# Grouped-MoE routing of a two-layer diffusion backbone: selection by pairwise comparison, row stores issued by SyncE

## The chip, the cores and the metric

The kernel runs on one core of a Trainium2 chip. The metric is the device time of one launch in microseconds (us); the kernel before takes 1316.8 us, the median of three runs (1316.08 to 1317.06). The engines are TensorE (PE), VectorE (DVE), ScalarE (ACT), GpSimd (POOL) and SyncE (SP). Each of them has a queue of instructions that it serves in order; DMAs are issued from such a queue, and in this kernel nearly all loads are issued by SP.

## The reference

Two layers run over 256 context tokens and 256 latent tokens of width 1024. A layer modulates its stream, projects it, runs two mixers (a gated linear recurrence and a neighbourhood attention), projects back with `w_out`, adds and normalizes, and then applies a mixture of 16 experts, which chooses two per token:

```python
def grouped_moe(h, w_router, b_router, w_gate_l, w_up_l, w_down_l):
    t = h.reshape(-1, shp[-1])                                   # tokens x 1024
    aff = sigmoid(t @ w_router)                                  # tokens x 16
    sel = (aff + b_router).reshape(n, 4, 4)                      # 4 groups of 4 experts
    group_score = lax.top_k(sel, 2)[0].sum(-1)                   # sum of the two best of each group
    g_idx = argmax(group_score)                                  # one group per token
    in_grp = sel[token, g_idx]
    local = lax.top_k(in_grp, 2)[1]                              # the two best experts of that group
    e_idx = g_idx * 4 + local
    gates = aff[e_idx] / sum(aff[e_idx])
    for e in range(16):                                          # w_gate, w_up 1024x512, w_down 512x1024
        hid = silu(t @ w_gate_l[e]) * (t @ w_up_l[e])
        out += combine[:, e:e+1] * (hid @ w_down_l[e])
```

Before it, `x = layer_norm(ALPHA*x + g1*y)` and `h = x*(1+sc2)+sh2`; behind it, another gated residual and layer norm. Layer 1 needs the latent tokens alone.

## The kernel before, in words

Tokens are treated in halves of 256: half 0 is the context, half 1 the latent tokens. Layer 0 has both, the first half's end overlapping the second half's matmuls; layer 1 has half 1 alone. Weights come in tiles of 1 MB (128 partitions x 2048 f32). Matrices that need precision are split into a high and a low part and multiplied in three matmuls (lines 426 to 428).

*Output projection.* For each half and each column tile of `w_out`, PE fills the bank `psy`, DVE adds the result to x, and `settle` (line 982) follows one column tile behind: `stat` accumulates sums of x and x squared by matmul into the bank `st`, and then x, scaled on ACT, is transposed by matmuls into the four banks `tr`. At the end of a half `owed` is emptied, one column tile after the other, each with its sums and its transposes.

*`ln1_end` (lines 1095 to 1145).* From `st` come mean and variance, from them the router's logits (`lg`), `aff`, and a small matrix `rT`. PE adds one matmul to each of the four `tr` banks, whose contents are then rows of h up to a factor. ACT evicts three of them to `hr` (line 1131), DVE the one of (n, j) = (1, 0) (line 1129), and each is stored to DRAM, to `hD`, from ACT's queue (line 1132).

*`route` (from 1148).* DVE computes which two experts each token takes: 25 small instructions on tiles of 128 x 16, 128 x 8 or 128 x 32 elements (lines 1170 to 1196, `sel` to `oh1`, `oh2` and their sum `m16`). PE counts places by a triangular matmul (`ppos`), DVE builds one-hot tiles (`oh`, line 1227, called `t` in the first half), PE turns them into lists of tokens (`ptb`, line 1231), and DVE writes these as `gidx` and `sums` (lines 1235, 1236). `by_load` sorts all but a few of the experts by load.

*`moe` (from 1304).* For each expert POOL gathers its rows of h from `hD` by an indirect DMA (`gather`, line 1345) into `xg`; the gather of a row needs both the indices and the stores. PE transposes them (`ptx`, line 1354), multiplies by gate and up (`pgA`, `pgB`, lines 1369 and 1379), then down (lines 1406 and 1412); POOL scatters the result (line 1433). Weights go to 16 slots of 1 MB, named `we` and `mw` after their pools; an expert takes four for gate and up (`in_wgu_dram`) and two for down (`in_wd_dram`), loaded by SP (line 1335). Of the first round, the slots from number NFREE on (14 in layer 0, 13 in layer 1) are held back: before their load POOL copies one element of the first gathered tile into the slot (line 1326), so the load follows the landing of the first gather. `fl` and `pfl` (lines 1521, 1523) are a flag on the last expert and its matmul.

What sets the order: a scheduler places the instructions of all engines when the kernel is built, from their dependencies; the order of the code decides among those that it could choose. Each engine then serves its queue in the order that came out.

Of the kernel before, what the change touches and what calls it, by code (L numbers as in the profile page):

```python
# [11 lines left out]
I32 = mybir.dt.int32  # L12
AF = mybir.ActivationFunctionType
# [5 lines left out]
P = 128  # L19
# [42 lines left out]
for _name, _w in (("sel4", 32), ("ident", 128), ("m0", 64), ("m1", 64), ("m2", 64), ("m4", 64), ("m8", 64), ("mM", 64),  # L62
                  ("cos", 256), ("sin", 256), ("tok", 4), ("c4", 8),
                  ("c32", 32), ("ord", 3 * NSORT), ("tri", 128), ("iota", CAP), ("rowtok", SEQ)):
    _C[_name] = (_n, _n + _w)
    _n += _w
# [4 lines left out]
def const_table():  # L71
# [28 lines left out]
    put("c32", np.broadcast_to(np.tile([4, 3, 2, 1], 8), (P, 32)))  # L100
# [85 lines left out]
class Emit:  # L186
# [740 lines left out]
    def w_out(self, l):  # L927
# [52 lines left out]
        def settle(xs, hf, st, tr, seen):  # L980
            self.stat(st, xs, seen)
# [14 lines left out]
        for half, c in order:  # L996
# [33 lines left out]
            if len(owed) > 1:  # L1030
                settle(*owed.pop(0))
            if (half, c) == order[0]:
                rows_of_g()
            if c == order[3 if hf == order[0][0] else -1][1]:
                while owed:
                    settle(*owed.pop(0))
# [56 lines left out]
    def ln1_end(self, hf, st, tr):  # L1093
# [29 lines left out]
        for n in range(2):  # L1123
            for j in range(2):
# [3 lines left out]
                if (n, j) == (1, 0):  # L1128
                    V.tensor_scalar(hr[:], tr[2 * n + j][:], s[:, 3, n:n + 1], None, op0=ALU.mult)
                else:  # L1130
                    S.activation(hr[:], tr[2 * n + j][:], AF.Copy, scale=s[:, 3, n:n + 1])
                S.dma_start(self.hD[128 * (n0 + n):128 * (n0 + n) + 128, 512 * j:512 * j + 512], hr[:])
# [14 lines left out]
    def route(self, hf, n0, aff):  # L1147
# [5 lines left out]
        sel, w1, w2 = (rt([P, 2, NE], x) for x in ("sel", "w1", "w2"))  # L1153
# [3 lines left out]


        grp = lambda x: x.rearrange("p t (g x) -> p (t g) x", g=4)
        s4 = sel[:].rearrange("p t (g x y) -> p (t g) x y", g=4, x=2)  # L1160
        gg = rt([P, 6, 8, 2], "gg")
        fl = lambda i, y: gg[:, i, :, y]
        wide = lambda x: x.unsqueeze(2).to_broadcast([P, 8, 4])
        t4 = lambda x: x.rearrange("p (t g) -> p t g", t=2)
        gm = rt([P, 4, 2], "gm")
        b4 = lambda x: x.unsqueeze(2).to_broadcast([P, 2, 4])
        g1 = rt([P, 2, NE], "g1")
        s44, wa, wb, wc = grp(sel[:]), grp(w1[:]), grp(w2[:]), grp(g1[:])
        c32 = self.cst("c32").rearrange("p (g x) -> p g x", x=4)
        V.tensor_tensor(gg[:, 0], s4[:, :, 0, :], s4[:, :, 1, :], op=ALU.max)  # L1170
        V.tensor_tensor(gg[:, 1], s4[:, :, 0, :], s4[:, :, 1, :], op=ALU.min)
        V.tensor_tensor(fl(2, 0), fl(0, 0), fl(0, 1), op=ALU.max)
        V.tensor_tensor(fl(2, 1), fl(0, 0), fl(0, 1), op=ALU.min)
        V.tensor_tensor(fl(3, 0), fl(1, 0), fl(1, 1), op=ALU.max)
        V.tensor_tensor(wa, s44, wide(fl(2, 0)), op=ALU.is_ge)
        V.tensor_tensor(fl(3, 0), fl(3, 0), fl(2, 1), op=ALU.max)
        V.tensor_tensor(wa, wa, c32, op=ALU.mult)
        V.tensor_tensor(fl(3, 1), fl(2, 0), fl(3, 0), op=ALU.add)
        V.tensor_reduce(fl(5, 0), wa, axis=AX.X, op=ALU.max)
        V.tensor_reduce(gm[:, 0], t4(fl(3, 1)), axis=AX.X, op=ALU.max)  # L1180
        V.tensor_tensor(wa, wa, wide(fl(5, 0)), op=ALU.is_equal)
        V.tensor_tensor(t4(fl(4, 0)), t4(fl(3, 1)), b4(gm[:, 0]), op=ALU.is_ge)
        V.scalar_tensor_tensor(wb, wa, -3e38, s44, op0=ALU.mult, op1=ALU.add)
        V.tensor_tensor(fl(4, 0), fl(4, 0), self.cst("c4"), op=ALU.mult)
        V.tensor_tensor(wb, wb, wide(fl(3, 0)), op=ALU.is_ge)
# [583 lines left out]
```

## Time and profile before

| | |
|---|---|
| median of 3 runs | 1316.8 us |
| the profiled execution's own time | 1317.83 us |
| its span | 1316.1 us |
| mean granted clock of TensorE | 0.958 |
| PE, PEld busy | 1199.3 us (91%), 747.6 us (57%) |
| DVE, ACT, POOL busy | 590.2 us (45%), 413.8 us (31%), 334.4 us (25%) |
| moved by DMA | 339.32 MB, mean 258 GB/s |

All times of rows are counted from the start of the span of one profiled execution, which took 1.0 us more than the median. PEld is the load of a matmul's weights, which overlaps PE. In a timeline, several instructions of one kind stand in one row (x8) with their common time; an engine's name with a q (SPq, ACTq) is the issue of a DMA from its queue; a bracket tells how long the engine was idle before, and which instruction or DMA released it as far as the semaphores show. "DMA to landing" is the time from the start of an issuing instruction's transfer to its completion. In a table of stretches, the granted clock stands as a share of 2.4 GHz (0.50 is 1.2 GHz), and the DMA share is the busy time of 16 DMA engines.

### The profile page before, as it was taken

What the parts mean: (1) busy time and instruction counts of PE and PEld (TensorE: products, weight loads), DVE (VectorE), ACT (ScalarE), POOL (GpSimd) and SP (SyncE); (2) the same over time, 40 slices, a digit from 0 to 9 for tenths busy, and PEclk for the clock granted to TensorE, in tenths of its full rate; (3) what the DMA queues carried; (4) which work ended last, traced back from release to release, by engine and by line L of the source; (5) the groups of instructions that cost most, each with busy time, mean ns of one, the idle gap of its engine ahead of it and who ended that gap; (6) DMA issues with size and microseconds to landing.
All of it is one profiled execution on the core that took longest, in us unless ns stands there. A gap on an engine that the chain in (4) does not pass through costs nothing. (4 is left out here: it accounts for less than half of the span.)

```text
span 1316.1 us, 22763 instructions
## 1 busy us (share of the span) xinstructions
PE 1199.3 (91%) x8919; PEld 747.6 (57%) x8919; DVE 590.2 (45%) x1397; ACT 413.8 (31%) x905; POOL 334.4 (25%) x349
## 2 busy tenths in 40 slices
PE   6989999988999799998997999998889899999984
PEld 4778767667788334333332688876667734333321
DVE  2466554786735414121111756364785524322214
ACT  2233254452544114111112653354345312001011
POOL 2233243323223101111000534353343311111001
PEclk9999999999999799999998999998999889999996
DMA  8794325313385799999998524354335799999993
GB/s 299 250 313 189 122 89 197 116 52 108 124 332 188 266 374 375 386 395 384 412 404 298 227 101 167 115 192 152 131 116 213 314 352 380 389 404 402 421 413 151
DMA packets 67684, 339.32 MB, mean 258 GB/s; under 512 B 10003, under 2 KB 17907, under 8 KB 31856
## 3 DMA queue, kind: packets, MB, share of 16 engines
q1 hardware_dynamic: 54016, 315.74, 62.1%
q0 software_dynamic: 5936, 12.58, 2.9%
q10 hardware_dynamic: 7616, 9.44, 2.2%
q8 instruction: 74, 1.21, 0.4%
q14 instruction: 42, 0.34, 0.1%
HBM read 322.80 MB, written 20.45 MB: 261 GB/s over the span
## 5 line engine op out<-in xcount | busy, mean ns | idle before, releaser
L422 POOL TENSOR_TENSOR wl<-w,wh 128x512 fp32r<-128x512 f32 x121 | 166.4, 1389 | 188.5 <-ACT wh L421 171.7
L1369 PE MATMUL pgA<-we,xgT 128*64 128x512 f32 x688 | 165.2, 613 | 2.7 <-DMA we<-in_wgu_dram 2.7
L426 PE MATMUL pscm<-xh,wh 128*128 128x512 f32 (+1 forms) x320 | 119.1, 376 | 3.3 <-ACT wh L421 2.3
L427 PE MATMUL pscm<-xl,wh 128*128 128x512 f32 (+1 forms) x320 | 120.7, 379 | 0.7 <-POOL xl L1603 0.5
L428 PE MATMUL pscm<-xh,wl 128*128 128x512 f32 (+1 forms) x320 | 118.6, 375 | 2.8 <-POOL wl L422 2.6
L421 ACT ACTIVATE wh<-w 128x512 fp32r<-128x512 f32 x160 | 96.5, 626 | 50.4 <-PE pscm L427 18.7
L1369 PEld LDWEIGHTS pgA<-we,xgT 128*64 128x64 f32 x688 | 48.1, 140 | 95.1 <-issue 84.9
L427 PE MATMUL pstm<-wl,xh 128*128 128x256 f32 x320 | 92.6, 290 | 3.4 <-DVE wl L422 1.8
L428 PE MATMUL pstm<-wh,xl 128*128 128x256 f32 x320 | 91.9, 287 | 0.0
L426 PE MATMUL pstm<-wh,xh 128*128 128x256 f32 x320 | 91.6, 287 | 0.0
L1433 POOL DMA_INDIRECT yD<-y,ss x25 | 23.0, 921 | 244.6 <-DVE y L1421 79.9
L1406 PE MATMUL pdA<-we,hdT 128*64 128x512 f32 x320 | 77.6, 619 | 3.3 <-DMA we<-in_wd_dram 3.2
L1369 PE MATMUL pgA<-mw,xgT 128*64 128x512 f32 x336 | 77.5, 598 | 0.0
L1360 DVE COPY xgT<-ptx 128x256 f32<-128x256 f32 (+1 forms) x32 | 15.4, 482 | 134.2 <-PE ptx L1354 91.1
L426 PEld LDWEIGHTS pscm<-xh,wh 128*128 128x128 f32 x320 | 61.3, 193 | 13.8 <-ACT wh L421 2.4
L428 PEld LDWEIGHTS pscm<-xh,wl 128*128 128x128 f32 x320 | 61.5, 193 | 12.5 <-POOL wl L422 3.4
L427 PEld LDWEIGHTS pscm<-xl,wh 128*128 128x128 f32 x320 | 61.9, 194 | 11.2 <-POOL xl L1603 1.6
L1387 DVE SCALAR_TENSOR_TENSOR hid<-hid,pgA 128x256 f32<-128x256 f32 x32 | 13.5, 421 | 115.2 <-ACT hid L1386 115.1
L427 PEld LDWEIGHTS pstm<-wl,xh 128*128 128x128 f32 x320 | 61.4, 192 | 5.4 <-POOL wl L422 2.2
L1386 ACT ACTIVATE hid<-pgA 128x256 f32<-128x256 f32 x32 | 12.3, 383 | 159.5 <-PE pgA L1369 159.5
L428 PEld LDWEIGHTS pstm<-wh,xl 128*128 128x128 f32 x320 | 61.5, 192 | 1.1 <-issue 0.8
L426 PEld LDWEIGHTS pstm<-wh,xh 128*128 128x128 f32 x320 | 61.4, 192 | 0.5
(394 smaller groups left out, 2358.9 us busy)
## 6 DMA issues: line engine op xcount, KB each, us to landing
we<-in_wgu_dram SPq DMA_DIRECT2D x86, 1024.0 KB
mw<-in_wgu_dram SPq DMA_DIRECT2D x42, 1024.0 KB
w<-in_wada_dram SPq DMA_DIRECT2D x41, 1024.0 KB
we<-in_wd_dram SPq DMA_DIRECT2D x40, 1024.0 KB
w<-in_win_dram SPq DMA_DIRECT2D x29, 1024.0 KB
mw<-in_wd_dram SPq DMA_DIRECT2D x24, 1024.0 KB
w<-in_wout_dram SPq DMA_DIRECT2D x11, 1024.0 KB
wa<-in_wada_dram SPq DMA_DIRECT2D x6, 1024.0 KB
```

The lines of the kernel that those rows point to most:

```text
L421: self.nc.scalar.activation(hi, src, AF.Copy)
L422: leng.tensor_tensor(lo, src, hi.bitcast(F32), op=ALU.subtract)
L426: mm(out, lh, rh, start=first, stop=False, **k)
L427: mm(out, lh, rl, start=False, stop=False, **k)
L428: mm(out, ll, rh, start=False, stop=last, **k)
L1360: V.tensor_copy(t[:, 0:4, :c], src)
L1369: mm(pA[64 * j:64 * j + 64, :], xgT[e][:, k, 0:64], wk[:, 512 * j:512 * j + 512], start=(k == 0), stop=(k == KT - 1), skip_group_check=Tru ...
L1386: S.activation(h, ps[:, :n], AF.Tanh, scale=0.5)
L1387: V.scalar_tensor_tensor(h, h, 1.0, ps[:, :n], op0=ALU.add, op1=ALU.mult)
L1406: mm(dA[64 * j:64 * j + 64, :], hdT[e][:, kb, 0:64], wk[:, 512 * j:512 * j + 512], start=(kb == 0), stop=(kb == 3), skip_group_check=True, ...
L1433: G.indirect_dma_start(out=self.yD[l][:], out_offset=bass.IndirectOffsetOnAxis(ap=idx, axis=0), in_=y[:c], in_offset=None, bounds_check=2 ...
```

## The change

- The selection is rewritten. Each expert is compared with the four of its group at once: two compares over 128 x (8 groups x 4 x 4) elements, "greater" and "greater or equal"; the latter replaces the former where the other expert stands earlier in the group (the constant `before`, which takes the place of `c32`), and the sum over the four is the expert's rank. The two of rank below 1.5 are the top two, their masked sum is the group's score, and the best group is found as before with `c4`. `m16` and `oh2` come straight from the rank, and `oh1` is their difference. There are 14 instructions instead of 25.
- All four rows of h of a half are evicted by ACT, and their stores are issued by SP instead of ACT.
- `settle` takes a list: at the end of a half the sums of all owed column tiles come ahead in the code of all their transposes, which are now in `turns`.
- The temporary tiles `w1` that `w3` and the last expert's flag use are now called `top`.

```diff
 _n = 0
 for _name, _w in (("sel4", 32), ("ident", 128), ("m0", 64), ("m1", 64), ("m2", 64), ("m4", 64), ("m8", 64), ("mM", 64),
                   ("cos", 256), ("sin", 256), ("tok", 4), ("c4", 8),
-                  ("c32", 32), ("ord", 3 * NSORT), ("tri", 128), ("iota", CAP), ("rowtok", SEQ)):
+                  ("before", 16), ("ord", 3 * NSORT), ("tri", 128), ("iota", CAP), ("rowtok", SEQ)):
     _C[_name] = (_n, _n + _w)
     _n += _w
 NCONST = _n
...
     put("iota", np.broadcast_to(np.arange(1, CAP + 1), (P, CAP)))
     put("tok", i[:, None] + 128 * np.arange(4)[None, :] - BIG)
     put("c4", np.broadcast_to(np.tile([4, 3, 2, 1], 2), (P, 8)))
-    put("c32", np.broadcast_to(np.tile([4, 3, 2, 1], 8), (P, 32)))
+
+    put("before", np.broadcast_to((np.arange(4)[None, :] < np.arange(4)[:, None]).reshape(-1), (P, 16)))
     put("sel4", (s % 32) == np.arange(32)[None, :])
     o = np.arange(NSORT)
     put("ord", np.broadcast_to(np.concatenate([o[::-1], o, o + NSTAT]), (P, 3 * NSORT)))
...
             self.R.update(uv=uv, gbr=gbr)
 
 
-        def settle(xs, hf, st, tr, seen):
-            self.stat(st, xs, seen)
+        def settle(jobs):
+            for xs, hf, st, tr, seen in jobs:
+                self.stat(st, xs, seen)
+            for job in jobs:
+                turns(*job)
+
+        def turns(xs, hf, st, tr, seen):
             for m, x, _ in xs:
                 rs = rt([P, 256], "rs", 2)
                 S.activation(rs[:], x, AF.Copy, scale=gb[:, m, 2 * hf:2 * hf + 1])
...
                 xs.append((m, x, w32[:, hf, m, :]))
             owed.append((xs, hf, st, tr, seen))
             if len(owed) > 1:
-                settle(*owed.pop(0))
+                settle([owed.pop(0)])
             if (half, c) == order[0]:
                 rows_of_g()
             if c == order[3 if hf == order[0][0] else -1][1]:
-                while owed:
-                    settle(*owed.pop(0))
+                settle(owed)
+                owed = []
                 if hf == 0:
                     self.ln1_end(hf, st, tr)
         return st, tr
...
                 hr = rt([P, 512], "hr", 4)
                 mm(tr[2 * n + j][:], rT[0:12, 128 * n:128 * n + 128], R["gbr"][0:12, 512 * j:512 * j + 512], start=False, stop=True,
                    skip_group_check=True)
-                if (n, j) == (1, 0):
-                    V.tensor_scalar(hr[:], tr[2 * n + j][:], s[:, 3, n:n + 1], None, op0=ALU.mult)
-                else:
-                    S.activation(hr[:], tr[2 * n + j][:], AF.Copy, scale=s[:, 3, n:n + 1])
-                S.dma_start(self.hD[128 * (n0 + n):128 * (n0 + n) + 128, 512 * j:512 * j + 512], hr[:])
+                S.activation(hr[:], tr[2 * n + j][:], AF.Copy, scale=s[:, 3, n:n + 1])
+                nc.sync.dma_start(self.hD[128 * (n0 + n):128 * (n0 + n) + 128, 512 * j:512 * j + 512], hr[:])
         if l == 1:
...
         NTL = self.T * P
         mm = nc.tensor.matmul
         ns = slice(n0, n0 + 2)
-        sel, w1, w2 = (rt([P, 2, NE], x) for x in ("sel", "w1", "w2"))
+        sel, rank = (rt([P, 2, NE], x) for x in ("sel", "rank"))
         oh1, oh2, gt = R["oh1"][:, ns], R["oh2"][:, ns], R["gt"]
         V.tensor_scalar(aff[:], aff[:], 0.5, 0.5, op0=ALU.mult, op1=ALU.add)
         V.tensor_tensor(sel[:], aff[:], self.br[:].unsqueeze(1).to_broadcast([P, 2, NE]), op=ALU.add)
 
-
         grp = lambda x: x.rearrange("p t (g x) -> p (t g) x", g=4)
-        s4 = sel[:].rearrange("p t (g x y) -> p (t g) x y", g=4, x=2)
-        gg = rt([P, 6, 8, 2], "gg")
-        fl = lambda i, y: gg[:, i, :, y]
-        wide = lambda x: x.unsqueeze(2).to_broadcast([P, 8, 4])
-        t4 = lambda x: x.rearrange("p (t g) -> p t g", t=2)
-        gm = rt([P, 4, 2], "gm")
-        b4 = lambda x: x.unsqueeze(2).to_broadcast([P, 2, 4])
-        g1 = rt([P, 2, NE], "g1")
-        s44, wa, wb, wc = grp(sel[:]), grp(w1[:]), grp(w2[:]), grp(g1[:])
-        c32 = self.cst("c32").rearrange("p (g x) -> p g x", x=4)
-        V.tensor_tensor(gg[:, 0], s4[:, :, 0, :], s4[:, :, 1, :], op=ALU.max)
-        V.tensor_tensor(gg[:, 1], s4[:, :, 0, :], s4[:, :, 1, :], op=ALU.min)
...
-        V.tensor_tensor(grp(oh1), wa, wide(fl(4, 1)), op=ALU.mult)
-        V.tensor_tensor(wb, wb, wide(fl(5, 1)), op=ALU.is_equal)
-        V.tensor_tensor(wc, wa, wb, op=ALU.add)
+        s4 = grp(sel[:])
+        by_j, by_i = s4.unsqueeze(2).to_broadcast([P, 8, 4, 4]), s4.unsqueeze(3).to_broadcast([P, 8, 4, 4])
+        cmp = self.mt([P, 256], "adasb", 4)
+        gt4, ge4 = (cmp[:, 128 * i:128 * i + 128].rearrange("p (g i j) -> p g i j", g=8, i=4) for i in range(2))
+        gt3, ge3 = (cmp[:, 128 * i:128 * i + 128].rearrange("p (g x) -> p g x", g=8) for i in range(2))
+        V.tensor_tensor(gt4, by_j, by_i, op=ALU.is_gt)
+        V.tensor_tensor(ge4, by_j, by_i, op=ALU.is_ge)
+        V.copy_predicated(gt3, self.cst("before").unsqueeze(1).to_broadcast([P, 8, 16]).bitcast(I32), ge3)
+        V.tensor_reduce(grp(rank[:]), gt4, axis=AX.X, op=ALU.add)
+
+        gg = rt([P, 3, 8], "gg")
+        gm = rt([P, 2, 2], "gm")
+        top = rt([P, 2, NE], "top")
+        t4 = lambda i: gg[:, i].rearrange("p (t g) -> p t g", t=2)
+        b4 = lambda i: gm[:, i].unsqueeze(2).to_broadcast([P, 2, 4])
+        V.scalar_tensor_tensor(top[:], rank[:], 1.5, sel[:], op0=ALU.is_lt, op1=ALU.mult)
+        V.tensor_reduce(gg[:, 0], grp(top[:]), axis=AX.X, op=ALU.add)
+        V.tensor_reduce(gm[:, 0], t4(0), axis=AX.X, op=ALU.max)
+        V.tensor_tensor(t4(1), t4(0), b4(0), op=ALU.is_ge)
+        V.tensor_tensor(gg[:, 1], gg[:, 1], self.cst("c4"), op=ALU.mult)
+        V.tensor_reduce(gm[:, 1], t4(1), axis=AX.X, op=ALU.max)
+        V.tensor_tensor(t4(2), t4(1), b4(1), op=ALU.is_equal)
+        mine = gg[:, 2].unsqueeze(2).to_broadcast([P, 8, 4])
 
         m16 = R["m16"]
-        V.tensor_tensor(grp(m16[:, ns]), wc, wide(fl(4, 1)), op=ALU.mult)
-        V.tensor_tensor(grp(oh2), wb, wide(fl(4, 1)), op=ALU.mult)
+        V.scalar_tensor_tensor(grp(m16[:, ns]), grp(rank[:]), 1.5, mine, op0=ALU.is_lt, op1=ALU.mult)
+        V.scalar_tensor_tensor(grp(oh2), grp(rank[:]), 1.0, mine, op0=ALU.is_equal, op1=ALU.mult)
+        V.tensor_tensor(oh1, m16[:, ns], oh2, op=ALU.subtract)
         pp = self.pb("ppos")
         for n in range(n0, n0 + 2):
             o = pp[:, NE * (n - n0):NE * (n - n0) + NE]
```

SP's queue around the routing of layer 0, before (`w_45` is the last tile of `w_out`, `we` and `mw` are slots of weights):

```order
L199 DMA w_45_4338<-in_wout_dram 128x2048
L1335 DMA we<-in_wgu_dram 128x2048 x5
L1335 DMA we<-in_wd_dram 128x2048 x2
L1335 DMA mw<-in_wgu_dram 128x2048 x4
L1335 DMA mw<-in_wd_dram 128x2048 x2
```

and after; the first four `hr` are the rows of the first half, the next four those of the second:

```order
L1135 DMA hD<-hr_3989 128x512
L1135 DMA hD<-hr_3993 128x512
L1135 DMA hD<-hr_3997 128x512
L1135 DMA hD<-hr_4001 128x512
L1328 DMA we<-in_wgu_dram 128x2048 x2
L1328 DMA we<-in_wd_dram 128x2048 x2
L1135 DMA hD<-hr_4465 128x512
L1135 DMA hD<-hr_4469 128x512
L1135 DMA hD<-hr_4473 128x512
L1135 DMA hD<-hr_4477 128x512
L1328 DMA mw<-in_wgu_dram 128x2048 x4
L1328 DMA mw<-in_wd_dram 128x2048 x2
```

The stores now stand in SP's queue, the second four of them ahead of four loads of gate and up weights and of the two held-back loads of down weights.

SP's queue around the routing of layer 1, before:

```order
L199 DMA w_81_10113<-in_wout_dram 128x2048
L1335 DMA we<-in_wgu_dram 128x2048 x8
L1335 DMA we<-in_wd_dram 128x2048 x2
L1335 DMA mw<-in_wgu_dram 128x2048 x3
L1335 DMA mw<-in_wd_dram 128x2048 x2
```

and after:

```order
L1328 DMA we<-in_wgu_dram 128x2048 x8
L1328 DMA we<-in_wd_dram 128x2048
L1135 DMA hD<-hr_10229 128x512
L1135 DMA hD<-hr_10233 128x512
L1135 DMA hD<-hr_10237 128x512
L1135 DMA hD<-hr_10241 128x512
L1328 DMA we<-in_wd_dram 128x2048
L1328 DMA mw<-in_wgu_dram 128x2048 x3
L1328 DMA mw<-in_wd_dram 128x2048 x2
```

The four stores stand ahead of the second load of the down weights and of the three gate and up loads, of which the last is held back.

PE's queue in layer 1 from the last of the index matmuls to the first expert, before:

```order
L1231 MATMUL ptb<-rr_10320,oh 96x2
L1523 LDWEIGHTS one_97
L1523 MATMUL pfl<-fl_1_11043,one_97 128x1
L1354 MATMUL ptx<-ct,xg_10410 128x96 x8
L1369 MATMUL pgA<-we,xgT_10423 64x512 x8
L1379 MATMUL pgB<-we,xgT_10423 32x256 x16
```

and after:

```order
L1224 MATMUL ptb<-rr_10287,oh 96x2
L1347 MATMUL ptx<-ct,xg_10377 128x96 x8
L1516 LDWEIGHTS one_97
L1516 MATMUL pfl<-fl_1_11010,one_97 128x1
L1362 MATMUL pgA<-we,xgT_10390 64x512 x8
L1372 MATMUL pgB<-we,xgT_10390 32x256 x16
```

The flag's matmul moves behind the eight transposes of the first gathered tile; the rest stands as it did.

At the ends of both halves that a routing waits for, PE's sums (`st`) and transposes (`tr`) stand in the order that they had. In the first half of layer 0, `ppos` stands six matmuls earlier, and a pair of transposes now lies among the matmuls of `ptb`.

## Rows read from the trace of the kernel before

**Rows 1.** Chain of waits, 1180 to 1300 us: share of each kind of piece.
```profile
by line: DMA we<-in_wgu_dram 33.9%; DMA mw<-in_wgu_dram 18.7%; DMA mw<-in_wd_dram 16.9%; DMA we<-in_wd_dram 13.5%; PE pdA L1406 6.2%; PE pgA L1369 5.8%; PE pfin L1658 1.7%; issue 1.3%; DVE zt L1646 0.7%; DVE y L1421 0.6%; PE ptx L1354 0.5%;
```

**Rows 2.** Stretches: length, busy of PE, PEld, DVE, ACT, POOL, PEclk, DMA, GB/s.
```profile
430.00:434.50 4.50, 2.01 (x10) 1.16 (x11) 3.52 (x30) 1.36 (x4) 0.70 (x1) 1.00 1.01 428
439.00:445.00 6.00, 2.25 (x27) 2.15 (x25) 4.77 (x24) 0.00 (x0) 2.40 (x2) 0.50 0.21 54
...
460.00:560.00 100.00, 100.00 (x805) 39.93 (x793) 28.58 (x61) 24.81 (x56) 10.52 (x11) 1.00 1.00 378
1066.00:1188.00 122.00, 122.00 (x930) 47.68 (x929) 37.24 (x77) 16.38 (x43) 15.14 (x16) 1.00 1.00 391
```

**Rows 3.** Timeline of SP, layer 0: start, duration, instruction.
```profile
421.33 0.85 SPq L1335 DMA_DIRECT2D mw<-in_wgu_dram  x2
...
425.96 0.33 SPq L1335 DMA_DIRECT2D mw<-in_wgu_dram  x1
...
445.24 0.90 SPq L1335 DMA_DIRECT2D mw<-in_wd_dram  x2
```

**Rows 4.** Timeline of POOL, layer 0, with idle time before and its releaser.
```profile
440.54 1.44 POOL L1345 DMA_INDIRECT xg<-hD,gidx  x1 [9.21 <-DVE sums L1236]
...
445.01 0.34 POOL L1326 COPY mw<-xg 96x1 f32<-96x1 f32 x2 [1.78 <-DMA xg<-hD,gidx]
```

**Rows 5.** Timeline of PE, layer 0, first transposes of the expert stage.
```profile
445.09 1.51 PE L1354 MATMUL ptx<-ct,xg 96*128 96x96 f32 x8 [2.06 <-DMA xg<-hD,gidx]
```

**Rows 6.** Timeline of DVE, layer 0, selection to indices.
```profile
432.70 0.17 DVE L1170 TENSOR_TENSOR gg<-sel 128x16 f32<-128x16 f32 x1
...
435.99 0.19 DVE L1195 TENSOR_TENSOR m<-g,gg 128x32 f16<-128x32 f32 x1
...
438.01 0.16 DVE L1235 TENSOR_TENSOR gidx<-ptb,sums 96x2 int32<-96x2 f32 x1
```

**Rows 7.** Timeline of ACT, layer 0, evictions and stores of h.
```profile
433.74 1.26 ACT L1131 ACTIVATE hr<-tr,lnst 128x512 f32<-128x512 f32 x2 [0.64 <-PE tr L1126]
434.45 1.66 ACTq L1132 DMA_DIRECT2D hD<-hr  x3
...
436.93 0.33 ACTq L1132 DMA_DIRECT2D hD<-hr  x1
```

**Rows 8.** Timeline of POOL, layer 1, first gather and copies.
```profile
1050.01 2.22 POOL L1345 DMA_INDIRECT xg<-hD,gidx  x1 [8.22 <-DVE oh L1227]
...
1055.34 0.59 POOL L1326 COPY mw<-xg 96x1 f32<-96x1 f32 x4 [1.83 <-DVE ids L1277]
```

**Rows 9.** Timeline of ACT, layer 1, evictions and stores of h.
```profile
1044.20 1.26 ACT L1131 ACTIVATE hr<-tr,lnst 128x512 f32<-128x512 f32 x2 [0.63 <-PE tr L1126]
...
1047.11 0.33 ACTq L1132 DMA_DIRECT2D hD<-hr  x1
```

**Rows 10.** Timeline of SP, layer 1, loads before the routing ends.
```profile
1031.37 0.33 SPq L1335 DMA_DIRECT2D we<-in_wd_dram  x1
...
1033.87 0.33 SPq L1335 DMA_DIRECT2D mw<-in_wgu_dram  x1
```

**Rows 11.** Tile xg: stretches 442 to 447, 447 to 700, 1058 to 1225 us.
```profile
DMA to landing us min/median/max: 4.5/4.5/4.5
...
DMA to landing us min/median/max: 7.0/8.5/9.7
...
DMA to landing us min/median/max: 7.4/7.5/8.4
```

**Rows 12.** Timeline of PE, layer 1, start of the expert stage.
```profile
1056.13 0.19 PE L1523 MATMUL pfl<-fl,one 128*128 128x1 f16 x1 [2.75 <-DVE fl L1521]
```

**Rows 13.** First half of layer 0: SP's loads, PE's stall, stretch after it.
```profile
383.08 2.09 SPq L1335 DMA_DIRECT2D we<-in_wgu_dram  x4
...
402.58 1.63 PE L1231 MATMUL ptb<-rr,t 128*96 128x2 f16 x31 [1.47 <-DVE t L1227]
...
404.00:407.00 3.00, 3.00 (x16) 1.97 (x16) 2.02 (x7) 0.26 (x1) 0.88 (x1) 0.50 0.00 0
```

More of the change, by code (lines that the diff above doesn't have):

```diff
@@ L1169, in route @@
-        c32 = self.cst("c32").rearrange("p (g x) -> p g x", x=4)
-        V.tensor_tensor(gg[:, 0], s4[:, :, 0, :], s4[:, :, 1, :], op=ALU.max)
-        V.tensor_tensor(gg[:, 1], s4[:, :, 0, :], s4[:, :, 1, :], op=ALU.min)
[L1172 to L1184, printed above, removed]
@@ L1185, in route @@
-        V.tensor_tensor(wb, wb, wide(fl(3, 0)), op=ALU.is_ge)
-        V.tensor_reduce(gm[:, 1], t4(fl(4, 0)), axis=AX.X, op=ALU.max)
-        V.tensor_tensor(wb, wb, c32, op=ALU.mult)
-        V.tensor_tensor(t4(fl(4, 1)), t4(fl(4, 0)), b4(gm[:, 1]), op=ALU.is_equal)
-        V.tensor_reduce(fl(5, 1), wb, axis=AX.X, op=ALU.max)
-        V.tensor_tensor(grp(oh1), wa, wide(fl(4, 1)), op=ALU.mult)
-        V.tensor_tensor(wb, wb, wide(fl(5, 1)), op=ALU.is_equal)
-        V.tensor_tensor(wc, wa, wb, op=ALU.add)
+        s4 = grp(sel[:])
@@ L1242, in route @@
             self.by_load(ptot)
-        w3 = rt([P, 2, NE], "w1")
+        w3 = rt([P, 2, NE], "top")
         for i, oh in enumerate((oh1, oh2)):
@@ L1504, in moe @@
                 self.glast = self.rt([P, 2, 2], "glast")
-                w = self.rt([P, 2, NE], "w1")
+                w = self.rt([P, 2, NE], "top")
                 mine = R["S"][:, r].unsqueeze(1).to_broadcast([P, 2, NSORT])
```

## The prediction, made before the changed kernel ran

> **What bounds the kernel now.** I read the chain of waits first, then the busy time in stretches around the two expert stages, then the instructions in order of time on SyncE (SP), GpSimd (POOL), ScalarE (ACT), VectorE (DVE) and TensorE (PE) around the one place where a stage waits for the routing. The chain ends in weight loads: the last 100 us before the output are one load behind another [rows 1]. The stretches say why. In layer 0 the DMA engines work until 434.5 us, then sink to a share of 0.21 between 439 and 445 us, and stand at 1.00 from 460 us on, with PE busy 100 of 100 us beside them; in layer 1 the same two ones stand in the row from 1066 to 1188 us [rows 2]. So from the moment the experts start, loads and PE both run without a gap, and what decides the end is when they start. A later start by x is a later end by about x, in each of the two layers.
>
> What starts them is the first gather of rows of h. In layer 0 the last free weight slots are filled at 425.96 us; the two held-back loads leave at 445.24 us, behind POOL's one-element copies at 445.01, which wait for the landed gather [rows 3, 4], and PE's first transpose starts at 445.09, released by that gather [rows 5]. The gather is issued at 440.54 and lands 4.47 us later.
>
> What does the gather wait for? Its indices are written at 438.01 [rows 6], 2.5 us before it starts. The last store of h is issued at 436.93 [rows 7], 3.6 us before. In layer 1 the gather starts at 1050.01 and the last store is issued at 1047.11, 2.9 us before [rows 8, 9]. I take it that the landing of the stores holds the gather, not the selection. The page of the profile names a DVE instruction as the releaser, so this is a reading and not a row.
>
> **The change part by part.** *Selection.* Before, m16 starts 435.99 - 432.70 = 3.3 us after the first max [rows 6], an eviction of h by DVE among it. The new chain has 11 steps up to m16, nearly all of them dependent. A small step takes 0.16 to 0.19 us [rows 6], so dependent ones start some 0.2 us apart, and for a tile of 128 elements, four times as wide as m16's, I estimate near 0.3 us: three wide steps and the step between the two compares make 1.2 us, seven small ones 1.4, together 2.6 us, so m16 comes 0.7 us earlier (bounds: 1.8 us if the new steps overlap like the old, 0 if the compares with doubled broadcasts run slow). With the stores holding the gather, this is worth nothing in the two critical places; were it the holder, it would be worth the same 0.7 us that I count for the stores next.
>
> *Stores by SP, evictions by ACT alone.* Two evictions on ACT take 1.26 us from 433.74, so four end near 436.2. Before, three DMA issues kept ACT from 434.45 to 436.11 and the fourth store left only at 436.93 [rows 7]. The last store is then issued some 0.75 us earlier in layer 0; in layer 1, where the first pair starts at 1044.20 and four would end near 1046.65, 0.45 us [rows 9]. That is the gain.
>
> The price is in SP's queue. It is served in order, and the four stores now stand ahead of four loads of expert 2's gate and up weights in layer 0. Before, these left between 421.33 and 425.96 us [rows 3] and were through when the DMA share fell, at 434.5. Now SP waits at the first store until 434.4 and issues the loads behind the last, at about 436.6. In layer 1 the second load of w_down and two gate and up loads, which left at 1031.4 to 1033.9 [rows 10], wait likewise until about 1047. PE doesn't need these weights before 460 us, so the bytes as such are hidden: they fill the hole in the DMA share. What they do is to fill it exactly while the gather runs.
>
> A gather that finds no loads lands 4.5 us after its issue; those that find loads in flight take 7.0 to 9.7, median 8.5, in layer 0, and 7.4 to 8.4, median 7.5, in layer 1 [rows 11]. So layer 0's first gather gets 4.0 us slower (bounds 0, if the loads don't reach it, and 5.2) and layer 1's 3.0 (bounds 0 and 3.9). I take the medians, since 4 MB at the 378 GB/s of rows 2 are 11 us, about what was in flight at the measured ones. Layer 0: -0.75 + 4.0 = +3.25 us for PE and for the held-back loads alike. Layer 1: the landing moves from 1055.34 [rows 8] by -0.45 + 3.0 = +2.55, and with it the held-back loads behind the copies. PE there started at 1056.13 with pfl, which waited for fl [rows 12]; pfl now stands behind the transposes, so PE starts at 1057.9, +1.7. PE paces the stage first and loads do at the end, so I take the middle, +2.1.
>
> The Trainium skill ("DMA: Bandwidth & Descriptors", section Queues, rings and completion order) says that a DMA engine goes round its queues and drains a whole packet of one before it turns to the next. With eight 8 KB pieces of a 1 MB load on each of 16 engines (same page, section The descriptor swizzle) and 378 GB/s, an estimate for one such packet is 2.8 us. The fastest loaded gather (7.0 us) agrees with one packet, the median with more. By one packet's wait for each first gather the sum would be +2.05 + 1.9 - 0.7 = +3.2 us instead of the one below; this is the third rival.
>
> *First half of layer 0.* Its route runs beside the second half's matmuls, but PE stalls 1.47 us there for the second one-hot tile, and soon after, from 404 to 407 us, works at a granted clock of 0.50, the 1.2 GHz level [rows 13]. m16 comes about 0.5 us earlier (DVE's eviction of psy stands between), the one-hots with it, and the new order puts a pair of transposes (0.3 us) into the stall; ACT, freed from DMA issues, has their operand in time. I take -0.7 us. Bounds: 0, and -2.2 if the 3 us at half clock run at full clock as well. The four stores there hold back one load, which left at 385 us as the last of four [rows 13]; the DMA engines have some 40 us for it before 434.5.
>
> *Sums taken ahead.* At the end of both critical halves PE's instructions stand in the same order as before, so this is worth 0. The smaller constant table and the later flag cost nothing on these paths: they lie beside PE's stream of matmuls.
>
> Sum: +3.25 + 2.1 - 0.7 = +4.65 us. The profiled execution took 1317.83 us (span 1316.1), 1.0 above the median of 1316.8; against its own time this gives 1322.5, and carried to the median 1321.5.
>
> **The rivals.** *The gather runs free.* If the loads behind the stores only begin to move when the first gather is nearly through, or don't hold it, only the gains are left: -0.75 in layer 0, -0.45 (loads) to -1.2 (PE, without pfl) in layer 1, -0.7 in the first half, together -2.3: 1314.5; with the half-clock stretch at full clock 1313.0. For it: stores and loads are in one queue, so the loads come last. Against it: the gather's descriptors take POOL 1.44 us [rows 4], and at 437 us 4 MB are ready to move. It decides from a gather landing under 5.2 us after its issue.
>
> *Only one layer's delay arrives.* If one stage has slack that the shares of 1.00 don't show (PE waiting for slots while loads are merely outstanding), the end moves by one term: +3.25 - 0.7 = +2.6 (1319.4) or +2.1 - 0.7 = +1.4 (1318.2). For it: a busy DMA share is no measure of bytes, which vary from 378 to 391 GB/s in rows 2. Against it: the critical chain in layer 1 is PE without a break and then loads without a break [rows 1, 2].
>
> *One packet's wait.* As worked out above, 1320.0.
>
> *The selection is the path after all.* Then m16's 0.7 us takes the place of the stores' 0.75 and 0.45, and the sum hardly differs, 1321.4; it makes no case of its own.
>
> **How the numbers follow.** About 2.6 us (0.2%) is what a measurement of this kernel can tell from no change. Forecast 0.50, centred on 1321.5, its own range 1318.5 to 1324.7 (the upper bounds together: +4.45 + 3.45 + 0). Free gather 0.23, half of it beyond -2.6 us. One layer 0.15, half of it within 0.2%. One packet 0.12, mostly slower. That makes faster 0.13, same 0.23, slower 0.64; for what I may have missed on the fast side I say 0.16, 0.22, 0.62. The range for 8 in 10 runs from 1313.8, inside the free gather with some luck on the clock, to 1325.
>
> **What would show it.** Right: SP's last store of layer 0 near 436.2 and four gate and up loads straight behind it; a DMA share near 1 from 437 to 447 us; a first gather that takes 7 us or more to land; POOL's copies and PE's first transpose near 448.5 (less the first half's gain), and near 1058 in layer 1; m16 0.7 us earlier without effect. Wrong: a first gather of 4.5 us beside those loads; a gather that starts with the indices and not with the stores; a stall in the first half that stays 1.47 us; or a shift at PE's first transpose that is gone by the next layer.

## The result, and the profile after

| | kernel before | changed kernel |
|---|---|---|
| median | 1316.93 us (4 runs) | 1326.27 us (4 runs) |
| range | 1316.08 to 1319.82 | 1325.51 to 1326.59 |
| ratio, 95% interval | | 1.0066 [1.0049, 1.0084] |
| the same on another chip (E5) | 1314.30 us (23 runs) | 1323.17 us (6 runs), 1.0070 [1.0045, 1.0096] |

The kernel became slower by 9 us. I had forecast 4.7 us, in a range that ended at 1325.0.

**The stores and the gather of layer 0.** SP's queue and POOL's after (start, duration, instruction, idle before it and releaser); they answer to [rows 3, 4].

```profile
424.19 0.33 SPq L1328 DMA_DIRECT2D we<-in_wd_dram  x1
437.78 2.05 SPq L1135 DMA_DIRECT2D hD<-hr  x4
439.93 2.15 SPq L1328 DMA_DIRECT2D mw<-in_wgu_dram  x4
```

```profile
443.24 1.33 POOL L1338 DMA_INDIRECT xg<-hD,gidx  x1 [8.64 <-DVE sums L1229]
...
452.28 0.31 POOL L1319 COPY mw<-xg 96x1 f32<-96x1 f32 x2 [6.44 <-DMA xg<-hD,gidx]
```

SP issues nothing for 13 us, then four stores, and right behind them the four loads. The gather then lands 9.04 us after its start, against 4.47 before; its landing is read here and below from the start of POOL's copies. The stretch in which the gather is out (columns as in [rows 2]) shows the DMA engines full, at a share of 0.96; before, it was 0.21 between 439 and 445 us.

```profile
443.00:452.00 9.00, 1.75 (x20) 1.65 (x19) 4.28 (x24) 0.00 (x0) 2.29 (x2) 0.50 0.96 350
```

Layer 1 is alike; the rows answer to [rows 8]. The gather takes 9.00 us, against at most 5.33 before: there the row of the copies names a DVE instruction (`ids`) as the last releaser, so the gather itself may have landed sooner.

```profile
1059.36 1.25 POOL L1338 DMA_INDIRECT xg<-hD,gidx  x1 [8.51 <-DVE oh L1220]
...
1068.36 0.54 POOL L1319 COPY mw<-xg 96x1 f32<-96x1 f32 x4 [6.46 <-DMA xg<-hD,gidx]
```

**What I had not followed: the flag in layer 0.** One row of SP's waits (line, what it waited for, us in total, times, longest), and SP's and DVE's timelines around it.

```profile
SPq L1518 <- DVE flag L1517: 17.4, 1, 17.4
```

```profile
515.69 6.64 SPq L1328 DMA_DIRECT2D we<-in_wgu_dram  x4
540.58 0.91 SPq L1328 DMA_DIRECT2D we<-in_wd_dram  x2
```

```profile
538.71 0.86 DVE L1418 COPY y<-pdB 32x256 f32<-32x256 f32 x2
539.61 0.16 DVE L1517 CAST flag<-pfl 128x1 int32<-128x1 f32 x1
```

SP reads the flag between two loads, and DVE writes it (`CAST`) at 539.61 us, behind the evictions of the fourth expert; PE's matmul `pfl` for it starts at 537.72, behind that expert's down-projection. Before, the cast stood among the instructions of the first expert:

```profile
446.71 0.14 DVE L1524 CAST flag<-pfl 128x1 int32<-128x1 f32 x1
```

SP's waits before have none for the flag. In the changed kernel SP issues no load from 522 to 540 us. The stretch of 40 us that begins 40 us behind the first expert's activation, before and after:

```profile
499.07:539.07 40.00, 40.00 (x310) 16.01 (x308) 16.15 (x32) 14.31 (x31) 5.06 (x6) 1.00 0.98 373
```

```profile
505.48:545.48 40.00, 40.00 (x311) 16.10 (x309) 16.30 (x33) 14.35 (x31) 4.97 (x6) 1.00 0.68 254
```

PE doesn't notice: it is busy 40 of 40 us in both. 0.30 of 40 us, 12 us of all DMA engines, are gone, and they are missed at the end of the layer, where between 698 and 733 us PE waits for loads eight times, 9.6 us together; the kernel before has no such wait of PE at the end of the layer. The longest, in PE's timeline after (`psada` is a sum with the weights `wa` that modulate the next layer):

```profile
730.18 1.94 PE L378 MATMUL psada<-wa,scw 128*32 128x256 f32 x16 [2.06 <-DMA wa<-in_wada_dram]
```

**Where the time went, by stages.** Each number below is the distance of two starts in one profiled execution. *Half*: from the last `psy` of the first half (DVE's add to x) to `sel` of the second half. *Gather 0*, *gather 1*: from `sel` to POOL's copies behind the landed gather, layers 0 and 1. *Experts 0*: from those copies to the first sum of squares of layer 1 (`rms`). *Front*: from there to `sel` of layer 1. *Experts 1*: from the copies to the last expert's activation. *Tail*: from there to DVE's last end.

| kernel | half | gather 0 | experts 0 | front | gather 1 | experts 1 | tail |
|---|---|---|---|---|---|---|---|
| before | 44.6 | 12.5 | 370.5 | 227.5 | 12.4 | 230.0 | 25.7 |
| changed | 46.1 | 16.5 | 378.6 | 221.2 | 16.4 | 228.1 | 23.0 |
| E5 changed, again | 45.4 | 16.8 | 378.0 | 220.9 | 16.9 | 227.6 | 22.9 |
| E7 first half on ACT | 44.9 | 16.8 | 378.8 | 221.2 | 16.9 | 227.9 | 22.9 |
| E6 flag read late | 44.6 | 16.8 | 367.8 | 221.0 | 17.7 | 227.4 | 22.9 |
| E10 ... and loads held, layer 1 | 44.9 | 16.8 | 368.5 | 220.9 | 11.7 | 234.9 | 22.8 |
| E9 ... and held in both | 46.4 | 12.0 | 374.2 | 223.3 | 12.3 | 234.0 | 22.8 |
| E1 stores on ACT | 44.9 | 12.4 | 371.9 | 224.8 | 12.0 | 227.8 | 25.7 |
| E12 the same, again | 44.9 | 12.2 | 370.3 | 223.5 | 11.8 | 227.6 | 22.7 |
| E8 selection alone | 44.5 | 13.6 | 372.2 | 221.5 | 12.1 | 227.7 | 23.4 |

*Front* lies between 220.8 and 227.5 and *tail* between 22.7 and 25.7 whatever was edited, and the start of the program up to the column *half* between 382 and 391 us, in all fifteen profiles. The kernel before was profiled at the long end of *front* and *tail*, the changed one 1.8 us late at the start. So the stages that I take to be moved by the change add up to more than 9 us: +1.5, +4.0, +8.1 and +4.0. I count *front* and *tail* as no part of the change, but this isn't shown for *front*: of the nine profiles whose second halves store from SP six have 220.8 to 221.2, and all six with the stores on ACT have 221.5 or more.

### The profile page after: what moved, and what is told of

It is laid out like the page before. It is cut to its first block, busy times and chain, and to the rows that moved or that the text cites. A ratio compares the mean times of both kernels' runs of the same rounds, so it can differ in the third digit from the quotient of the medians.

```text
span 1324.8 us, 22735 instructions
## 1 busy us (share of the span) xinstructions
PE 1196.1 (90%) x8919; PEld 746.4 (56%) x8919; DVE 588.4 (44%) x1361; ACT 415.8 (31%) x908; POOL 332.7 (25%) x349
## 5 line engine op out<-in xcount | busy, mean ns | idle before, releaser
L1379 ACT ACTIVATE hid<-pgA 128x256 f32<-128x256 f32 x32 | 12.3, 385 | 165.4 <-PE pgA L1362 165.4
## 6 DMA issues: line engine op xcount, KB each, us to landing
mw<-in_wgu_dram SPq DMA_DIRECT2D x42, 1024.0 KB, 12.4
```

The lines of the kernel that those rows point to most:

```text
L1379: S.activation(h, ps[:, :n], AF.Tanh, scale=0.5)
```

## The experiments

Each ran in five rounds against the kernel before on its chip; the ratio is the recorded estimate from all runs, with its 95% interval, and isn't quite that of the medians given beside it (E6: 1.0017, the medians give 1.0009). Between chips the ratio of the same kernel differed by up to 0.13%.

**E1, stores back on ACT.**

```diff
-                nc.sync.dma_start(self.hD[...], hr[:])
+                S.dma_start(self.hD[...], hr[:])
```

> The changed kernel with one edit: the four stores of h are issued from ACT's queue again; selection, ACT's four evictions and the list of settle stay changed. SP's queue is then that of the kernel before, loads and flag alike. Theory A (the move of the stores to SP is the whole loss, by loads beside the gather and by the flag that the move displaces): first gathers land 4.3 to 5.3 us after their start, SP doesn't wait for the flag, 1315 to 1318 us. Rival B (the new selection or the evictions cost time of their own, the longer one-hot step and half-clock stretch of the first half among it): 1319 to 1323 us, with the first gathers at 4.5 us.

Measured: 1311.41 us, 0.9983 [0.9957, 1.0008]. One line takes the whole loss back: the gathers land after 4.27 and 4.46 us, the cast of layer 0's flag stands at 445.67, and SP waits for no flag. Theory A holds, rival B falls. The line undoes two effects at once, though, so the next ones part them.

**E2, the flag's block moved ahead in the code.**

```diff
-            if e == 3:
+            if e == 0:
                 fl16 = self.rt([P, 1], "fl16", 1, F16)
```

> The changed kernel with one edit: the block that computes the flag stands at the first expert in the code instead of the fourth, so that its cast on DVE comes before the adds of the next layer norm, as in the kernel before; stores stay on SP. Theory A: SP's wait of 17.4 us for the flag in layer 0 goes, the DMA share between 500 and 550 us is back at 0.97 or more, the last experts of layer 0 don't wait for loads; gathers still land 8 to 10 us after their start; 1322 to 1325 us, 1.5 to 4 below the changed kernel. Rival C (the loads lost in that wait are made up anyway before layer 1): the same time within 1 us.

Measured: 1323.95 us, 1.0092 [1.0064, 1.0120]. The edit failed to do what it was for: the cast came at 484.01 instead of 539.61, behind the evictions of an earlier expert, and SP read the flag earlier as well, so it stood 13.6 us in layer 0 and 12.8 us in layer 1. On the flag it decides nothing; E6 replaced it. It does show what the gather waits for: in layer 1 the indices came 6.2 us after `sel`, in the changed kernel 4.8, and the gather started no later for it than in other kernels with stores on SP, 7.6 us after `sel`.

**E3, the kernel before with ACT's evictions and SP's stores.**

```diff
-                S.dma_start(self.hD[...], hr[:])
+                nc.sync.dma_start(self.hD[...], hr[:])
```

> The kernel before with two edits: all four rows of h evicted by ACT, stores issued by SP; old selection, old settle. Theory A: as slow as the changed kernel, 1324 to 1328 us, with gathers at 8 to 10 us in both layers and the late flag. Rival B (selection): 1317 to 1321 us.

Measured: 1335.47 us, 1.0168 [1.0137, 1.0199], beyond what any theory expected. Gathers of 9.59 and 9.60 us and a wait for the flag of 17.4 us are there as in the changed kernel, and SP's queue has the same order, so the slowdown needs no new selection. But it is 1% slower than that: *gather 0* (17.3) and *gather 1* (16.9) are 1.4 us longer together than in the changed kernel, *experts 0* (380.3) 1.7. The two profiles lie 9.5 us apart, and most of the rest stands in *front* (224.7, 3.6 us longer), *tail* (25.6, 2.6) and *experts 1* (229.5, 1.4); why, stays open.

**E4, E2 with the four loads behind the stores held in layer 0 until the gather has landed.**

```diff
-NFREE = 14, 13
+NFREE = 10, 13
```

> The kernel of the early flag with one more edit: in layer 0 the loads from slot 10 on, not 14, are held until the first gather has landed (the four gate and up loads that stand behind the stores in SP's queue); layer 1 is unchanged and serves as control. Theory A (loads in flight slow the gather): layer 0's first gather lands 4.3 to 5.5 us after its start, layer 1's stays at 8 to 10; PE's first transpose in layer 0 comes 3.5 to 4.5 us earlier than with the early flag alone; the time falls by less, 0 to 4 us, since 4 MB of loads now start later. Rival D (stores issued by SP land late themselves, whatever follows them): layer 0's gather stays at 8 to 10 us.

POOL's timeline, layer 0 and layer 1 of the same execution:

```profile
440.71 1.56 POOL L1338 DMA_INDIRECT xg<-hD,gidx  x1 [8.41 <-DVE sums L1229]
...
445.46 0.66 POOL L1319 COPY mw<-xg 96x1 f32<-96x1 f32 x5 [1.92 <-DMA xg<-hD,gidx]
...
1049.99 1.97 POOL L1338 DMA_INDIRECT xg<-hD,gidx  x1 [8.88 <-DVE oh L1220]
...
1060.23 0.54 POOL L1319 COPY mw<-xg 96x1 f32<-96x1 f32 x4 [6.36 <-DMA xg<-hD,gidx]
```

4.75 us where the loads were held, 10.24 where they were not, both with stores from SP; in E2, where layer 0 didn't hold them, its gather took 8.65. So the loads behind the stores slow the gather, not the stores' queue: theory A, and rival D falls. The whole: 1321.39 us, 1.0061 [1.0036, 1.0087], against 1.0092 for E2 on the same chip.

**E5, the changed kernel again**, without an edit.

> The changed kernel once more, unedited, on the same chip as the next three, as their reference and as a second profile. By all theories 1.004 to 1.010 of the kernel before; the early stretch before 362 us, 1.6 us late in its first profile, should show whether that was chance: within 0.7 us of the kernel before if so, 1 to 2 us late if the smaller constant table does it.

Measured: 1.0070 [1.0045, 1.0096]; its start up to the last `psy` of the first half took 385.3 us, against 387.9 before and 389.7 in the first profile. So the 1.8 us at the start were chance.

**E6, the flag read behind all experts.** The instructions of PE, DVE, ACT and POOL stand in the order that they have in the changed kernel; only the reading moves.

```diff
                 V.tensor_copy(flag[:], pfl[:, 0:1])
-                fv = nc.values_load(flag[0:1, 0:1], min_val=0, max_val=P)
...
+        fv = nc.values_load(flag[0:1, 0:1], min_val=0, max_val=P)
         with self.tc.If(fv):
```

> The changed kernel with one edit: the flag is read by the engines behind all experts of a layer, not among them; nothing else moves on any engine. SP's wait of 17.4 us in layer 0 goes for certain. Theory A (SP's stop costs DMA time that layer 0's end and the loads behind it miss): DMA share of the 40 us it stood in back from 0.68 to 0.98 or more, the last experts and the sums with the next layer's weights 3 to 8 us earlier against the first expert, 2 to 6 us off the total against the changed kernel. Rival C (layer 1's front gives it back): within 1 us of the changed kernel.

Measured: 1315.50 us, 1.0017 [0.9996, 1.0038], against 1.0070 for E5 on the same chip: the stop is worth 0.53%, 7 us, known to some 0.3% from the two intervals. The stretch that answers to the pair above, and the sums with the next layer's weights:

```profile
502.98:542.98 40.00, 40.00 (x311) 16.11 (x309) 16.30 (x33) 14.33 (x31) 4.97 (x6) 1.00 0.99 376
```

```profile
705.25 3.66 PE L378 MATMUL psada<-wa,scw 128*32 128x256 f32 x64
```

Theory A, a little above its upper end; rival C falls. PE has no wait for a load left there. *Experts 0* is 10 us shorter than in E5, and 2 to 4 us shorter than in the kernels with stores on ACT. I put those 2 to 4 us down to the four loads beside the gather: they fill DMA time that stands empty before, and the end of the layer comes sooner for it; E9 against E10 below bears this out.

**E7, the first half's stores on ACT, the others on SP.**

```diff
-                nc.sync.dma_start(self.hD[...], hr[:])
+                (nc.sync if hf else S).dma_start(self.hD[...], hr[:])
```

> The changed kernel with one edit: the stores of layer 0's first half are issued by ACT, those of the second halves by SP. Theory A (ACT, free of the issues, splits the next tile of w_out earlier, POOL's part of it then overlaps DVE's one-hot tiles and slows both, and PE stands and runs at half clock for longer): the pair of one-hots takes 3.4 us again instead of 4.5, the selection of the second half starts 1.2 to 1.6 us earlier against the last eviction of psy of the first half; 1 to 2 us off the total against the changed kernel. Rival E (the 1.5 us are the clock's chance): nothing moves.

DVE and POOL in the changed kernel, and in E7:

```profile
400.26 4.50 DVE L1220 TENSOR_TENSOR t<-iota,q 128x1536 f16<-128x1536 f16 x2
...
401.24 4.66 POOL L423 TENSOR_TENSOR wl<-w,wh 128x512 fp32r<-128x512 f32 x2 [6.31 <-PE psy L428]
```

```profile
395.84 3.43 DVE L1220 TENSOR_TENSOR t<-iota,q 128x1536 f16<-128x1536 f16 x2
...
398.99 2.66 POOL L423 TENSOR_TENSOR wl<-w,wh 128x512 fp32r<-128x512 f32 x2 [8.48 <-ACT wh L422]
```

The mechanism is as theory A has it: with ACT free of the issues, POOL's split starts a microsecond into the one-hots instead of near their end, and both take longer. The time is not: 1.0082 [1.0056, 1.0108], within the noise of E5, and *half* is 44.9 against 45.4. In the six profiles in which the first half stores from SP (the changed kernel, E2 to E6), with 4.50 to 4.52 us for the one-hots, *half* lies at 44.6 to 46.1; in the other nine, with 3.43, at 44.5 to 44.9, but for E9 with 46.4.

What goes with *half* is the granted clock and not the one-hots. Between 392 and 417 us PE has the clock of 0.50 for 3.4 us in nine profiles, and *half* is 44.5 to 44.9; for 6.8 us in the six others, and *half* is 45.4 to 46.4. Of the kernels with the slow one-hots E6 is among the first, of those with the fast ones E9 among the second (stretches of E6 and of E9):

```profile
406.50:412.50 6.00, 6.00 (x40) 6.00 (x39) 1.90 (x7) 1.35 (x3) 0.00 (x0) 0.72 0.52 178
```

```profile
406.50:412.50 6.00, 6.00 (x34) 4.96 (x34) 1.94 (x10) 0.74 (x2) 1.23 (x1) 0.50 0.38 123
```

So the collision is shown, and where the shorter stretch went with it, in E6, *half* is as long as before (44.6). Five of six profiles have the longer stretch with it and one of nine without it; that it makes that stretch more likely isn't shown.

**E8, the new selection alone in the kernel before.**

```diff
-        V.tensor_tensor(gg[:, 0], s4[:, :, 0, :], s4[:, :, 1, :], op=ALU.max)
...
+        V.tensor_tensor(gt4, by_j, by_i, op=ALU.is_gt)
...
```

> The kernel before with the new selection alone (evictions, stores and settle as before; with settle's list the instructions of all engines would stand in the same order). Theory A (the stores hold the gather, so m16's 0.5 to 0.8 us are worth little): 0.997 to 1.001 of the kernel before. Rival B (the new selection costs): over 1.002.

Measured: 1311.53 us, 0.9985 [0.9962, 1.0009]: theory A. Here m16 started 4.45 us after `sel`, later than before (3.52): DVE's eviction of h still stands in between, and DVE, there sooner, waits 0.97 us for PE's `tr`. The gather started 8.24 us after `sel`, against 8.07, though its indices came 0.9 us later.

**E9, E10: all three causes removed, stores of the second halves on SP** (flag as in E6, first half as in E7; E10 holds loads in layer 1 alone).

```diff
-NFREE = 14, 13
+NFREE = 10, 10      # E9
+NFREE = 14, 10      # E10
```

> The changed kernel with the stores of the second halves still on SP, and three edits: the flag read behind the experts, loads held until the first gather has landed from slot 10 on in both layers, the first half's stores on ACT. Theory A (the queue that issues the stores costs nothing by itself; what stands behind them does): first gathers land 4.2 to 5.5 us after their start in both layers, no wait for the flag, 0.997 to 1.003 of the kernel before. Rival D (a store from SP is slow in itself): over 1.003.

> As the kernel with all three edits, but with loads held from slot 10 on in layer 1 alone; in layer 0 the four loads stay beside the gather. Theory A: layer 0's gather 8 to 9.5 us, and in return the end of layer 0's experts and of the loads for layer 1's modulation 3 us earlier against the first expert, as in the kernel with the flag read late; layer 1's gather 4.2 to 5.5 us; 0.995 to 1.001 of the kernel before.

Measured: 1.0015 [0.9989, 1.0042] and 1.0014 [0.9991, 1.0036]. The gathers behave as expected: 4.26 and 4.49 us in E9, 9.25 and 4.05 in E10. What I hadn't expected is that holding buys nothing. E10 against E6: *gather 1* 6.0 us shorter, *experts 1* 7.6 longer. E9 against E10: *gather 0* 4.8 shorter, *experts 0* 5.6 longer. I read this as the DMA engines being the limit of both stages: time that SP leaves them empty is paid by the gather or by the loads, as one likes. Whether a store from SP costs anything besides, the interval doesn't exclude.

**E11, stores on ACT and the flag read late; E12 and E13, E1 and E11 again on one chip.** Edits as in E1 and E6.

> The changed kernel with all stores on ACT and the flag read behind the experts: the candidate for a version that beats both. As SP waits for no flag where the stores are on ACT, theory A says that the late read is worth nothing here: 0.996 to 1.000 of the kernel before, like the kernel with the stores on ACT alone (0.9983).

> The changed kernel with the stores on ACT, once more: 0.996 to 1.000 of the kernel before by all theories. From the end of the last expert of layer 0 to the first sums of layer 1 (122.1 us before, 123.6 in the first run of this kernel) 122 to 124.5 us.

> The same with the flag read behind the experts, on the same chip. Theory F (the order at the end of layer 0 is worth 2 us or more): 0.992 to 0.996, and 2 us or more below the kernel with the early read, with the stretch from the last expert of layer 0 to the first sums of layer 1 at 120 to 121.5 us again. Theory G (chance): within 1.5 us of that kernel.

Measured: E11 1305.32 us, 0.9943 [0.9919, 0.9966]; E12 1309.53 us, 0.9970 [0.9944, 0.9996]; E13 1308.69 us, 0.9950 [0.9929, 0.9971]. Both versions are well ahead of the changed kernel. With the early read the gain over the kernel before is 0.2 to 0.3%, selection and ACT's evictions once the stores stay on ACT; the interval of E1 still holds no gain, that of E12 doesn't. Whether the late read adds to it stays open: the medians of E12 and E13 lie 0.84 us apart, as chance (G) has it, but their ratios 0.20%, 2.6 us, as theory F has it, and E11 lies below E1, and below the 0.996 that was expected, as well. The stretch from the last expert's activation to layer 1's first sums, 121.9 and 121.5 us, doesn't part them.

## Why the prediction was wrong

The direction was right, and so was the mechanism on which it stood; the size was half of what came, because one step was priced at nothing that cost 7 us, and other terms had errors that partly cancel: layer 0's delay mostly came back, layer 1's was larger, and the gain of the first half didn't come.

- *"The smaller constant table and the later flag cost nothing on these paths: they lie beside PE's stream of matmuls"*: this is the step that failed. I followed the flag in layer 1, where it moved by eight transposes, and asked whether PE waits for it. In layer 0 its matmul moved behind the down-projection of the fourth expert, and the engine that waits is SP, which reads the flag between two loads, for 17.4 us. E6 prices it at 0.53%, 7.0 us of the 9. The move of the flag is itself a consequence of the stores' queue: with the stores on ACT (E1) it stands early again, with the old selection and the stores on SP (E3) it stands late.
- *Selection, m16 0.7 us earlier, worth nothing*: right. `sel` to m16 took 3.52 us before and 2.85 after; E8 shows that the gather doesn't start with the indices.
- *The last store 0.75 and 0.45 us earlier*: right for the store, not for the gather. From `sel` to the end of the last issue: 4.79 and 4.08 us in layer 0, 4.50 and 4.02 in layer 1. The gather follows the last issue by 3.3 and 3.4 us in layer 0, by 2.6 and 3.3 in layer 1, which fits what I read from [rows 7, 9]: the stores hold it, as E2 and E8 show. But in layer 1 the gain doesn't reach the gather, which starts 7.08 us after `sel` before and 7.37 after; in layer 0 it is 8.07 and 7.49. In layer 1 the gather follows the start of the last issue by 3.5 to 4.1 us in all nine profiles with stores from SP and by 2.9 to 3.0 in the six with stores from ACT; whether the queue does this or what stands behind the stores isn't separated.
- *The gather 4.0 and 3.0 us slower beside the loads*: right, 4.57 and at least 3.67; E4 shows that it is the loads. (The 4.5 of [rows 11] is the second gather of layer 0, since the first starts before that stretch; the first one's 4.47 is from [rows 4].) Counted from `sel`, the sum for layer 0 (+3.25) measured +4.0, the landing in layer 1 (+2.55) +4.0. The rival of one packet's wait falls with these numbers, as does the free gather.
- *Layer 0's delay arrives at the end*: half wrong. The loads that delay the gather are ahead by 4 MB, and the layer ends on loads: with the flag out of the way *experts 0* gives 2.5 to 4.1 us of some 4.5 back (E6 against E12 and E1). Layer 1's delay arrives, 5.7 to 5.9 us in the same pairs: *experts 1* is equal in the three. The rival "only one layer's delay arrives" describes E6, 1.0017, best, though E6's interval holds the forecast's own 1321.5 too (a ratio of 1.0036).
- *First half, -0.7 us*: it didn't come; *half* is 0.0 to 1.5 us longer than before in the six profiles with its stores on SP. m16 came 0.56 us earlier, as said (3.99 us after `sel` before, 3.43 after). But that ACT is free earlier was counted as a gain alone; it starts POOL's split beside DVE's one-hots, which then take 4.50 us instead of 3.43. PE stands 1.12 us instead of 1.47 [rows 13], but later. What made *half* 1.5 us longer in the changed kernel is the stretch at a granted clock of 0.50 that follows, 6 us in the row below and 3 in [rows 13]; it isn't tied to the one-hots (E7).

```profile
406.00:412.00 6.00, 6.00 (x35) 4.96 (x34) 1.89 (x9) 0.10 (x1) 0.00 (x0) 0.50 0.47 161
```

- *Sums taken ahead, worth nothing*: no run has this part alone, so it rests on PE's sums and transposes standing in the order that they had.
- The change holds a gain as well, selection and evictions together 0.2 to 0.3%, 2 to 4 us (E1, E12). I had priced the selection at nothing and the evictions, with the stores, at 0.75 and 0.45 us; where the rest comes from isn't shown.

Put together from the ratios: selection, evictions and settle -0.2 to -0.3% (E1, E12); stores on SP without the flag +0.3 to +0.5% (E6 against E1 and E12); the flag +0.53% (E5 against E6). The sum must give E5's 0.70%, since each piece is a difference between neighbours in one chain of kernels; it parts the loss and is no check of it. What stays open: the 1% by which E3 is slower than the changed kernel, the shorter *front* of most kernels with stores on SP, and what sets the length of the slow stretch in the first half.

## What to carry to other kernels

Before an instruction that waits is put into the queue that issues the loads, list everything behind it: SP stood 13 us for the evictions and the loads then ran against the gather. Where a scheduler orders the program, look for every instruction that has moved relative to the load queue, also one that the change doesn't touch, and ask of each value that the load queue itself reads when it is written: the DMA share over a stretch (0.98 against 0.68) shows such a stop where the busy time of PE shows nothing. And where DMA engines are full through a stage, time for which they stand empty before comes due at its end: here 12 us empty, and 9.6 us of PE's waits for loads.

## What the runs showed of the hardware

A gather of 96 rows landed 4.05 to 5.33 us after its start where no weight loads were in flight, and after 8.65 to 10.34 us beside 3 or 4 MB of them, in all fifteen profiles (landings read from POOL's copies, so upper bounds). The Trainium skill ("DMA: Bandwidth & Descriptors", section Queues, rings and completion order), by which an engine drains a packet of one queue before it turns to the next, gave an estimate of 2.8 us more; 4.6 and at least 3.7 were measured in the changed kernel, more than one packet's wait.

Two one-hots on VectorE of 128 x 1536 (f16) took 3.43 us together where GpSimd began the first of its two tensor_tensor 1.67 us behind their start or later (nine profiles), and 4.50 to 4.52 where it began 0.96 to 1.38 us behind it (six profiles). In the changed kernel, counted from the start of the one-hots, VectorE's first ended at 1.76, GpSimd's first at 2.89, VectorE's second at 4.50 and GpSimd's second at 5.63; GpSimd's two took 4.66 us instead of the 2.66 of E7. The Trainium skill ("SBUF — State Buffer", section SBUF: two separate sides) says that a VectorE instruction with two SBUF inputs and a GpSimd instruction that reads SBUF share one port pair, which the one that starts first holds for its whole instruction. The rows agree: the four ends follow one another, 1.1 to 1.6 us apart.
